# A hybrid encoder layer: another order of work at its start, and loads, stores and transposes moved around its far attention

## The chip, the cores and the metric

The kernel runs on one core of one Trainium2 chip. A core has a matrix engine (TensorE, here PE, with its weight loads as PEld), a vector engine (DVE), a scalar engine (ACT), GpSimd (POOL) and SyncE (SP); transfers are issued from the queues of SP, ACT and POOL and run on 16 DMA engines that they share. Every engine works through its own instructions in the order in which they were written, and waits for the others by semaphores. The metric is the device time of one execution in microseconds (us), as the median of several runs; less is better. Beside it stands one execution taken with the profiler, whose span and trace the text reads.

## The reference

One layer of an encoder over 2048 tokens of width 1024, with a memory of 256 tokens, all in float32:

```python
y = rmsnorm(h, norm_mix_g[l]) @ w_in[l]
q, k, v = ...                       # 8 heads of 64, partial rotary on q and k
att = dilated_sliding_attention(q, k, v)      # windows (128, 1), (512, 4), (2048, 16)
conv = conformer_conv(a, g, conv_w[l], conv_b[l], conv_ln_g[l], conv_ln_b[l])
                                    # a * sigmoid(g), 31 taps a channel, layernorm, silu
h = h + concatenate([att, conv]) @ w_out[l]
h = h + cross_attention(rmsnorm(h, norm_x_g[l]), rmsnorm(mem, norm_mem_g[l]))
h = h + square(relu(rmsnorm(h, norm_mlp_g[l]) @ w_up[l])) @ w_down[l]
return rmsnorm(h, norm_final_g)
```

The three outputs of the dilated attention are added with weights that come from their log denominators.

## The kernel before

**Arithmetic.** Each product of float32 matrices is made of three matmuls with a high and a low part of either side: high by high, high by low, low by high (`mm3`, L268 to L270). So each weight tile and each chunk of activations is split first: ACT casts the high part, DVE or POOL subtracts to get the low part. For the first stage these are f16 parts of weights that were scaled by a power of two; the scale comes from the sum of squares (`wscale`: ACT squares a 128x1024 tile at L207, PE adds over the partitions at L212, DVE works out the power of two), and `scaled_split` (L224 to L226) scales, casts and subtracts.

**The start (about 0 to 70 us).** `setup` (L154) loads seven small vectors in POOL's queue into one tile, `vecs`; PE transposes it (`pvec`, L163), and a short chain through DVE and PE (`pgain`, L254) gives `gmix`, the mixer's gain scaled by a power of two. `xprep` (L392) prepares 512 tokens of x, block n of four: it loads them in eight tiles (`xn`), ACT adds up their squares (`ssx`, L380), POOL and DVE make the reciprocal root (`rsx`), PE spreads it over the partitions (`rb`), ACT copies it (`rbs`, L400). Then for each of eight chunks of 128 columns PE transposes four tiles into a PSUM bank (`xt`, L405; two banks), DVE copies it (`xts`, L407; eight buffers) for a store to DRAM in SP's queue (`xscr`), DVE multiplies by gain and root (`xv`, L410; two buffers), ACT casts (`xh`) and POOL subtracts (`xl`). `glu_first` (L641) makes the first four units of the convolution's input from these chunks: g0, a0, g1, a1, each eight chunks by three matmuls of 512 columns. Its order is written by hand at the place where the stage is set up (L911 to L957): generators are advanced one step at a time, and a pin (`after`, `behind`, `pinned`) keeps an engine's next instructions behind a named earlier one. SP's queue also holds zeros for the edges of two DRAM tensors (`uscr`, `vtok`), the mask, and the next weights (`lraw`, `raw_v`).

**The linear stage (to about 400 us)** makes the rest of the gated units, q, k and v, and the convolution's first block on DVE.

**The far stage (about 400 to 700 us)** is the attention of the first 512 tokens with all three windows, four pairs of heads. Two windows' results go to DRAM (`oscr`), are loaded again (`ld`) and combined on DVE and POOL (`combine`, L1077 on). Between the attention's steps PE works through a list of other steps, `filler` (L1315): eight steps of the gated units of the later blocks at a time, and the folding of the cross attention's matrices (`Matrices`), where `turn` (L522) transposes weights of four heads on PE in four steps a head (`xqt`, L531), each copied by ACT and subtracted by DVE (`wlo_m`, L534).

**After it** comes the dense part: `wpost` (L1286) loads and splits the weights of the output projection (`raw_o`, `whi_o`, `wlo_o`; two raw buffers), of the cross attention and the MLP, while DVE and PE make the near attention of the next block.

Of the kernel before, what the change touches and what calls it, by code (L numbers as in the profile page):

```python
# [21 lines left out]
P = 128  # L22
# [25 lines left out]
def hybrid_layer(ctx, tc, A, out):  # L48
# [105 lines left out]
    def setup():  # L154
# [8 lines left out]
        PE.transpose(pv[:, 0:64], vecs, ident[0:64, 0:64])  # L163
        ACT.copy(gv, pv[:, 0:64])
        g8 = gv[:, GV["mix"]:GV["mix"] + 8]
# [3 lines left out]
        pg = ps("c", "pgain")  # L169
        bcast_rows(pg, top_[:, 0:1], 1)  # L170
        DVE.tensor_reduce(top_[:, 1:2], pg[:, 0:P], axis=AX.X, op=ALU.max)
# [4 lines left out]
        DVE.tensor_scalar(gmix, g8, top_[:, 4:5], None, op0=ALU.mult)  # L176

    def conv_weights():
        cwn = t2("cwn", F32, (32, DCONV))
        DVE.memset(cwn, 0.0)  # L180
# [42 lines left out]
    def scaled_split(raw, c, hi, lo, eng):  # L223
        ACT.activation(raw, raw, AF.Copy, scale=c)  # L224
        ACT.copy(hi, raw)
        eng.tensor_tensor(lo, raw, hi, op=ALU.subtract)  # L226
# [11 lines left out]
    def rstd_col(dst, ss_ps, n, stat):  # L238

        v = stat.tile([P, 8], F32, tag="st_v", name="st_v", bufs=2)  # L240
        t = stat.tile([P, 8], F32, tag="st_t", name="st_t", bufs=2)
        DVE.tensor_scalar(v[:, :n], ss_ps, 1.0 / D, EPS, op0=ALU.mult, op1=ALU.add)  # L242
        newton_rsqrt(dst, v[:, :n], t[:, :n])

    def newton_rsqrt(dst, v, t):
        POOL.tensor_tensor(dst, v, mhalf.to_broadcast([P, v.shape[1]]), op=ALU.pow)  # L246
        DVE.tensor_tensor(t, dst, dst, op=ALU.mult)
        DVE.scalar_tensor_tensor(t, t, -0.5, v, op0=ALU.mult, op1=ALU.mult)
        DVE.scalar_tensor_tensor(dst, t, 1.5, dst, op0=ALU.add, op1=ALU.mult)

    def bcast_rows(dst_ps, col, n):

        for j in range(n):
            PE.transpose(dst_ps[:, j * P:(j + 1) * P], col[:, j:j + 1].to_broadcast([P, P]), ident)  # L254

# [119 lines left out]

    def sumsq(sp, t, ss, j, n):

        for e in range(2):
            q = sp.tile([P, 512], BF16, tag="junk", name="junk", bufs=1)
            last["sumsq"] = ACT.activation(q, t[e], AF.Square, accum_out=ss[:, n * e + j:n * e + j + 1])  # L380

    def rstd_nat(sp, nat, name):
        n = len(nat)
        ss = sp.tile([P, 8], F32, tag="ss", name=f"ss{name}", bufs=2)
        for j in range(n):
            sumsq(sp, nat[j], ss, j, n)
        r = sp.tile([P, 4], F32, tag="rs", name=f"rs{name}", bufs=2)
        DVE.tensor_tensor(ss[:, 0:n], ss[:, 0:n], ss[:, n:2 * n], op=ALU.add)
        rstd_col(r[:, 0:n], ss[:, 0:n], n, sp)
        return r  # L390

    def xprep(sp, n):  # L392
        xtiles(n)
        nat = [load_nat(sp, A["x"][0, 512 * n + P * j:512 * n + P * (j + 1), :], f"xn{n}_{j}", q=nc.gpsimd if n > 1 else None) for j in range(4)]
        yield
        r = rstd_nat(sp, nat, f"x{n}")
        rb = ps("c", f"rb{n}")
        bcast_rows(rb, r, 4)
        rbs = sp.tile([P, 512], F32, tag="rbs", name=f"rbs{n}", bufs=1)
        ACT.copy(rbs, rb)  # L400
        yield
        for k in range(KC):
            pt = ps("a", f"xt{n}_{k}")
            for j in range(4):
                PE.transpose(pt[:, j * P:(j + 1) * P], nat_cols(nat[j], k), ident)  # L405
            xt = sp.tile([P, 512], F32, tag="xt", name=f"xts{n}_{k}", bufs=8)
            DVE.tensor_copy(xt, pt)  # L407
            dma(xscr[k][:, 512 * n:512 * (n + 1)], xt)
            xv = sp.tile([P, 512], F32, tag="xv", name=f"xv{n}_{k}", bufs=2)
            DVE.scalar_tensor_tensor(xv, pt, gmix[:, k:k + 1], rbs, op0=ALU.mult, op1=ALU.mult)  # L410
            last[f"x{n}_{k}"] = ACT.copy(XH_[k, n], xv)
            POOL.tensor_tensor(XL_[k, n], xv, XH_[k, n], op=ALU.subtract)
            yield
# [5 lines left out]
    def memory(sp):  # L419
# [23 lines left out]
        for i, t in enumerate((*mh, *ml)):  # L443
            dma(f(mscr[i]), f(t), nc.gpsimd)
        r = rstd_nat(sp, nat, "m")
        DVE.tensor_copy(rmem[:, 0:2], r[:, 0:2])
# [162 lines left out]
    def glu(c, ns, fine=False):  # L609
# [31 lines left out]
    def glu_first(sp, ns):  # L641
# [9 lines left out]
        for x, c in units:  # L651
# [3 lines left out]
                     for q in ("hi", "lo")]  # L655
            scaled_split(raw[nm], kept_scale[nm][0], *w[nm], POOL)
            if x == "a":
                DVE.tensor_scalar(cwu[:, c], cw[:, c], kept_scale[nm][1], None, op0=ALU.mult)
            yield
        for n in ns:  # L660
            for x, c in units:
# [3 lines left out]
                if x == "g":  # L665
                    sig = t2(f"sig{c}_{n}")
                    ACT.activation(sig, pt, AF.Tanh, scale=kept_scale[f"g{c}"][1])
                else:
                    u = t2(f"u{c}_{n}")
                    last["dve"] = DVE.scalar_tensor_tensor(u, sig, 1.0, pt, op0=ALU.add, op1=ALU.mult)  # L670
                    dma(uscr[c][:, 15 + 512 * n:15 + 512 * (n + 1)], u)
                yield
# [238 lines left out]
    with ExitStack() as st:  # L911
        sp = pool("stage", stack=st)
        setup()
        four = glu_first(sp, (0, 1))
# [8 lines left out]
        next(four)  # L923
        cwt = conv_weights()
        next(cwt)
        next(x0)
        behind("sumsq", four)
        drain(x0)
        with ExitStack() as st0:
            after(st0, "x0_3")  # L930
            drain(cwt)
        for _ in range(3):
            behind("x0_3", four)
        behind("x0_5", x1)
        for _ in range(6):
            behind("sumsq", four)
        early01 = (0, 1)
# [9 lines left out]
        steps = pipeline(*units, lin_v(hook), stage={0: 4})  # L947
        behind("x0_7", steps)
        drain(islice(steps, 6))
        weave(islice(steps, 24), (x1, 0.5))  # L950
        drain(x1)
        mem = memory(sp)
        later = pinned(chain(xprep(sp, 2), islice(mem, 1), xprep(sp, 3), mem), "x1_7")
        qks = pinned(qkscale(), "x1_7")
# [187 lines left out]
    def att_units(p, far, then):  # L1142
# [25 lines left out]
        def unit(pr, hh, pat, g, k, q_, opt, o0):  # L1168
# [139 lines left out]
    with ExitStack() as st:  # L1308
# [6 lines left out]
        def filler():  # L1315
# [691 lines left out]
```

## Time and profile before

| what | value |
|---|---|
| time, median of 3 runs | 2806.13 us (2802.68 to 2808.23) |
| the profiled execution's own time | 2799.84 us |
| its span | 2798.1 us |
| mean granted PE clock | 0.991 |
| busy: PE, DVE, ACT, POOL | 96%, 68%, 45%, 21% of the span |
| DMA | 535.68 MB, mean 191 GB/s |
| chain that ended last | PE 68%, issue 9%, DMA 8%, DVE 7%, ACT 3%, POOL 3%, SP's queue 2% |

The text reads the page, and from the trace a timeline (each row an instruction, or several alike, with its start, its duration, engine, line and operation, output and inputs; in brackets how long the engine was idle ahead of it and what ended that), a table of windows with each engine's busy time, and groups of instructions by line. A matmul's duration in a row reaches into the next one's, since they are pipelined: two matmuls of 512 columns whose rows say 0.38 start 0.215 us apart.

### The profile page before, as it was taken

How to read it: one execution, taken by the hardware profiler on the slowest of the kernel's cores; microseconds unless marked ns; L12 is line 12 of the kernel's file. 1: busy time of each engine (PE TensorE's matmuls, PEld its weight loads, DVE VectorE, ACT ScalarE, POOL GpSimd, SP SyncE). 2: the span in 40 equal slices, each digit the busy share in tenths (PEclk: the TensorE clock that was granted, in tenths of full speed). 3: DMA queues.
4: the chain of work that ended last, by engine and by line, in shares of the span. 5: the costliest groups of instructions: out<-in, count | busy, mean ns of one | idle time of the engine just before them, and what ended most of it. 6: DMA issues, size and time to landing. Idle time of an engine off the chain costs nothing.

```text
span 2798.1 us, 40584 instructions
## 1 busy us (share of the span) xinstructions
PE 2692.8 (96%) x14783; PEld 2072.3 (74%) x14783; DVE 1905.7 (68%) x3475; ACT 1271.6 (45%) x2171; POOL 583.6 (21%) x798
## 2 busy tenths in 40 slices
PE   6999999998899999999999999999999999999998
PEld 3544457876678888788888888887887788878887
DVE  4568826664689866578986578666475776666765
ACT  5842217655345333434544443454344444444435
POOL 5564313543002212200111201121010122100000
PEclk9999999999899999999999999999999999999999
DMA  9765557887535676767467766764534554584553
GB/s 273 209 184 114 142 165 203 245 240 226 174 120 185 199 233 201 236 217 218 139 190 222 254 207 217 234 235 136 165 124 132 188 199 150 174 300 152 165 184 106
DMA packets 468776, 535.68 MB, mean 191 GB/s; under 512 B 98172, under 2 KB 339440, under 8 KB 468576
## 3 DMA queue, kind: packets, MB, share of 16 engines
q1 hardware_dynamic: 431536, 412.03, 48.8%
q0 software_dynamic: 35312, 117.81, 11.8%
q10 hardware_dynamic: 1728, 3.24, 0.3%
q8 instruction: 116, 1.90, 0.3%
q14 instruction: 84, 0.69, 0.1%
HBM read 384.46 MB, written 148.52 MB: 190 GB/s over the span
## 4 chain that ended last, share of the span: by engine, by line
PE 68%; issue 9%; DMA 8%; DVE 7%; ACT 3%; POOL 3%; SPq 2%; POOLq 0%; ACTq 0%; DVEq 0%
PE b L1705 8%; PE dn L268 4%; PE dn L269 4%; PE dn L270 4%; PE up L268 3%; PE up L270 3%; PE up L269 3%; SPq L57 2%; PE lin L269 2%; PE lin L270 2%; PE lin L268 2%; PE pt L994 2%; PE s L1187 2%; PE x L269 1%; PE x L268 1%
## 5 line engine op out<-in xcount | busy, mean ns | idle before, releaser
L285 DVE SCALAR_TENSOR_TENSOR cacc<-cu,cwu,cacc 128x512 f32<-128x512 f32 x480 | 393.5, 821 | 6.4
L988 ACT ACTIVATE sm<-sm,o 128x256 f32<-128x256 f32 (+1 forms) x384 | 160.1, 467 | 118.3 <-DVE o L987 118.2
L268 PE MATMUL dn<-hhh,whi_d 128*128 128x512 f32 x512 | 201.9, 404 | 4.3 <-ACT hhh L1542 3.3
L268 PE MATMUL up<-mh,whi_u 128*128 128x512 f32 x512 | 203.9, 398 | 0.0
L269 PE MATMUL dn<-hhl,whi_d 128*128 128x512 f32 x512 | 200.7, 394 | 0.9 <-DVE hhl L1543 0.9
L270 PE MATMUL up<-mh,wlo_u 128*128 128x512 f32 x512 | 200.0, 391 | 0.0
L269 PE MATMUL up<-ml,whi_u 128*128 128x512 f32 x512 | 199.7, 390 | 0.0
L270 PE MATMUL dn<-hhh,wlo_d 128*128 128x512 f32 x512 | 199.6, 393 | 0.0
L987 DVE CUSTOM_DVE_ANT_0 sm<-s,mask 128x256 f32<-128x256 f32 (+1 forms) x384 | 126.9, 374 | 45.3 <-DMA oscr<-o 16.9
L246 POOL TENSOR_TENSOR nr<-st_v,mhalf 128x4 f32<-128x4 f32 x12 | 13.5, 1128 | 630.7 <-DVE st_v L242 630.7
L998 DVE TENSOR_TENSOR pl<-pt,ph 128x512 f16<-128x512 f32 x160 | 109.6, 685 | 49.6 <-ACT ph L997 49.2
L1557 DVE TENSOR_TENSOR h<-h,dn 128x512 f32<-128x512 f32 x128 | 86.4, 683 | 71.1 <-PE dn L270 70.7
L997 ACT CAST ph<-pt 128x512 f16<-128x512 f32 x160 | 92.6, 579 | 80.5 <-PE pt L994 79.9
L268 PEld LDWEIGHTS dn<-hhh,whi_d 128*128 128x128 f32 x512 | 95.6, 189 | 23.4 <-ACT hhh L1542 4.3
L270 PEld LDWEIGHTS dn<-hhh,wlo_d 128*128 128x128 f32 x512 | 96.7, 189 | 20.4
L269 PEld LDWEIGHTS dn<-hhl,whi_d 128*128 128x128 f32 x512 | 96.8, 189 | 19.7 <-DVE hhl L1543 1.8
L270 PEld LDWEIGHTS up<-mh,wlo_u 128*128 128x128 f32 x512 | 96.1, 188 | 20.5
L268 PEld LDWEIGHTS up<-mh,whi_u 128*128 128x128 f32 x512 | 96.2, 188 | 18.7
L269 PEld LDWEIGHTS up<-ml,whi_u 128*128 128x128 f32 x512 | 96.3, 188 | 18.5
L268 PE MATMUL o<-cath,whi_o 128*128 128x512 f32 x256 | 103.9, 406 | 5.2 <-ACT whi_o L259 4.5
L270 PE MATMUL o<-cath,wlo_o 128*128 128x512 f32 x256 | 102.2, 401 | 1.5 <-DVE wlo_o L260 1.5
L268 PE MATMUL x<-pth,whi_b 128*128 128x512 f32 x256 | 100.4, 398 | 2.4 <-ACT xp L1466 1.4
(622 smaller groups left out, 7982.1 us busy)
## 6 DMA issues: line engine op xcount, KB each, us to landing
raw_u<-in_w_up_dram SPq DMA_DIRECT2D x64, 512.0 KB
raw_d<-in_w_down_dram SPq DMA_DIRECT2D x64, 512.0 KB
k<-kscr SPq DMA_DIRECT2D x32, 640.0 KB
raw_a<-ascr SPq DMA_DIRECT2D x32, 512.0 KB
raw_b<-bscr SPq DMA_DIRECT2D x32, 512.0 KB
lou<-wlo_u POOLq DMA_DIRECT2D x32, 512.0 KB, 5.5
lod<-wlo_d POOLq DMA_DIRECT2D x32, 512.0 KB, 5.5
wlo_u<-lou SPq DMA_DIRECT2D x32, 512.0 KB
```

The lines of the kernel that those rows point to most:

```text
L57: (q or nc.sync).dma_start(o, i)
L268: PE.matmul(o, lh, rh, start=first, stop=False)
L269: PE.matmul(o, lh, rl, start=False, stop=False)
L270: last["pe"] = PE.matmul(o, ll, rh, start=False, stop=end)
L285: DVE.scalar_tensor_tensor(acc, u[:, t:t + 512], cwu[:, c, t:t + 1], acc, op0=ALU.mult, op1=ALU.add)
L987: last["dve"] = DVE.tensor_tensor_reduce(dst, so, mask[:, 256 * m:256 * m + nk], 1.0, 3e38, ALU.add, ALU.min, mn)
L988: last["act"] = ACT.activation(dst, dst, AF.Exp, bias=mn, scale=-1.0)
L994: last["pe"] = PE.transpose(pt[:, j, :], sm[:, j, :], ident)
L997: ACT.copy(ph, pt)
L998: DVE.tensor_tensor(pl, pt, ph, op=ALU.subtract)
L1557: last["dve"] = DVE.tensor_tensor(hs[m], hs[m], pt, op=ALU.add)
L1705: PE.matmul(o, w[i][:, k, :], Y[b][q][k], start=first and k + x == 0, stop=k == 3 and x == 2, skip_group_check=not first)
```

## The change

Four things are changed.

1. **The first 70 us.** The load of the convolution's weights (`cwn`) goes ahead of the vectors' loads. `gv` is copied by DVE, not ACT. The transposes of x's first chunks, and the root of x's first block, are pinned behind the vectors' chain, and DVE's copies `xts` behind `rsx0`. The low part of g0's weights is made by DVE, not POOL. The squares of x's second block are made in single steps between the chunks of the first. g0 and a0 go by turns over the chunks of the first block, in two PSUM banks, with the start of g1 between them; the scaled taps (`cwu`) follow a unit's end. The weights of the gated units that come next (`glu` with the first two blocks) are loaded in POOL's queue, not SP's; x's third block is loaded after the first block's last chunk. In SP's queue the zeros, the mask and `raw_v` thereby come ahead of all stores of x's first block.
2. **The last far store** (`oscr` of the fourth pair of heads) is issued by ACT, not SP.
3. **The output weights** 2 to 7 of the first block (`raw_o`) are loaded in POOL's queue, not SP's.
4. **The filler** takes two gated steps after each of the four steps of `turn`, where it took eight after the fourth.

The diff's core (the hand-written order at its end is cut):

```diff
-        ACT.copy(gv, pv[:, 0:64])
+        DVE.tensor_copy(gv, pv[:, 0:64])
...
+            with ExitStack() as st:
+                after(st, "rsx0")
+                DVE.tensor_copy(xt, pt)
...
-            dma(raw, wcols(w_in, c0), nc.gpsimd if fine else None)
+            dma(raw, wcols(w_in, c0), nc.gpsimd if fine or ns[0] == 0 else None)
...
-            scaled_split(raw[nm], kept_scale[nm][0], *w[nm], POOL)
+            scaled_split(raw[nm], kept_scale[nm][0], *w[nm], DVE if nm == "g0" else POOL)
...
+        pts = [ps("mm", f"lin{x}") for x in "ga"]
+        runs = [linear_steps(pts[i], *w[f"{x}0"], 0) for i, x in enumerate("ga")]
+        for i in (0, 0, 0, 0, 1, 0, 1, 1, 0, 1, 0, 1, 1, 0, 1, 1):
+            next(runs[i], None)
+            yield
+        for i, x in enumerate("ga"):
+            finish(x, 0, 0, pts[i])
...
+        cwt = conv_weights()
+        next(cwt)
         setup()
...
+        x0, x1 = pinned(x0, "pgain", "gain"), pinned(x1, "pgain", "gain")
         next(x0)
-        behind("sumsq", four)
+        behind("sumsq", pinned(four, "rsx0"))
...
-                    os_.rearrange("p b h e -> p b (h e)"), None if far else nc.scalar)
+                    os_.rearrange("p b h e -> p b (h e)"), None if far and pr < 3 else nc.scalar)
...
-        dma(raw, src)
+        dma(raw, src, nc.gpsimd if name[0:2] == "o0" else None)
...
-                yield from mats.turn(h)
-                yield from islice(gated, 8)
+                for _ in mats.turn(h):
+                    yield
+                    yield from islice(gated, 2)
```

PE's first rows before, from the last pair of x's first transposes on:

```order
L405 MATMUL xt_0_487<-ident,xn_3_0_402 128x128
L405 MATMUL xt_1_499<-ident,xn_3_0_402 128x128
L163 MATMUL pvec<-ident,vecs 128x64
L254 MATMUL pgain<-ident,gtop 128x128
L254 MATMUL rb_475<-ident,rsx_466 128x128 x4
L405 MATMUL xt_2_511<-ident,xn_0_0_390 128x128
```

And of the change, from PE's second row on:

```order
L213 MATMUL sqs_g_441<-sqv_g_439,small 128x1
L163 MATMUL pvec<-ident,vecs 128x64
L255 MATMUL pgain<-ident,gtop 128x128
L409 MATMUL xt_0_497<-ident,xn_0_0_392 128x128
L409 MATMUL xt_0_497<-ident,xn_1_0_396 128x128
L409 MATMUL xt_0_497<-ident,xn_2_0_400 128x128
```

`pvec` and `pgain` were behind the eight transposes of chunks 0 and 1, and are ahead of them now; `rb` follows those transposes.

ACT before, at about 43 to 54 us, where the root of x's second block (`rbs_636`) and the first weights of the next units (`lraw_g_669`, `lraw_a_681`) meet:

```order
L224 ACTIVATE fraw_a_434<-fraw_a_434,wscl 128x1024
L207 ACTIVATE sqj_a_694,sqv_a_695<-lraw_a_681 128x1024
L400 COPY rbs_636<-rb_631 128x512
L224 ACTIVATE lraw_g_669<-lraw_g_669,wscl 128x1024
L225 CAST fhi_a_663<-fraw_a_434 128x1024
```

And of the change, at the same place (`rbs_650`, `lraw_g_679`, `lraw_a_691`):

```order
L225 ACTIVATE fraw_a_436<-fraw_a_436,wscl 128x1024
L226 CAST fhi_a_674<-fraw_a_436 128x1024
L667 ACTIVATE sig_0_789<-ling,wscl 128x512
L667 ACTIVATE sig_0_856<-lin,wscl 128x512
L404 COPY rbs_650<-rb_645 128x512
L208 ACTIVATE sqj_g_681,sqv_g_682<-lraw_g_679 128x1024
L417 CAST xh_1_410<-xv_0_670 128x512
L208 ACTIVATE sqj_a_705,sqv_a_706<-lraw_a_691 128x1024
```

The root's copy stood behind a square that needs `lraw_a`, and stands ahead of both squares now.

SP's queue in the far stage, before, around the loads for the combine of the second pair of heads (`ld`; `v_02` are the values of the third pair):

```order
L57 DMA qh_5_6019<-qscr 64x2048
L57 DMA ql_3667<-qscr 64x2048
L57 DMA ld_6073<-oscr_2_89 128x4x132
L57 DMA ld_6073<-oscr_1_88 128x4x132
L57 DMA v_02_5999<-vtok 128x1x260 x5
```

And of the change:

```order
L57 DMA v_02_5999<-vtok 128x1x260 x7
L57 DMA ql_3667<-qscr 64x2048
L57 DMA v_02_5993<-vtok 128x1x260 x5
L57 DMA ld_6071<-oscr_1_88 128x4x132
L57 DMA ld_6071<-oscr_2_89 128x4x132
```

The two `ld` loads went behind five loads of values.

More of the change, by code (lines that the diff above doesn't have):

```diff
@@ L169, in setup @@
         pg = ps("c", "pgain")
-        bcast_rows(pg, top_[:, 0:1], 1)
+        last["pgain"] = bcast_rows(pg, top_[:, 0:1], 1)
         DVE.tensor_reduce(top_[:, 1:2], pg[:, 0:P], axis=AX.X, op=ALU.max)
@@ L224, in scaled_split @@
         ACT.activation(raw, raw, AF.Copy, scale=c)
-        ACT.copy(hi, raw)
+        last["split"] = ACT.copy(hi, raw)
         eng.tensor_tensor(lo, raw, hi, op=ALU.subtract)
@@ L374, in nat_cols, with sumsq, rstd_nat @@
         return t[k // 4][:, (k % 4) * P:(k % 4 + 1) * P]
[L376 to L382, printed above, removed]
+    def sumsq(sp, t, ss, j, n, e):
+        q = sp.tile([P, 512], BF16, tag="junk", name="junk", bufs=1)
+        last["sumsq"] = ACT.activation(q, t[e], AF.Square, accum_out=ss[:, n * e + j:n * e + j + 1])
+    def rstd_nat(sp, nat, name, steps=False):
         n = len(nat)
@@ L395, in xprep @@
         yield
-        r = rstd_nat(sp, nat, f"x{n}")
+        r = yield from rstd_nat(sp, nat, f"x{n}", n == 1)
         rb = ps("c", f"rb{n}")
-        bcast_rows(rb, r, 4)
+        last[f"rbt{n}"] = bcast_rows(rb, r, 4)
         rbs = sp.tile([P, 512], F32, tag="rbs", name=f"rbs{n}", bufs=1)
-        ACT.copy(rbs, rb)
+        last[f"rb{n}"] = ACT.copy(rbs, rb)
         yield
@@ L664, in glu_first @@
                     yield
[L665 to L671, printed above, removed]
+                finish(x, c, n, pt)
                 yield
```

78 lines of the change are left out of this document (53 added, 25 removed).

## The prediction

> **What bounds the kernel now.** The page's busy table comes first, then a table of windows (start:end, length, and for PE, PEld, DVE, ACT and POOL busy time with instruction count; then the granted PE clock, the DMA share and GB/s).
>
> ```profile
> PE 2692.8 (96%) x14783; PEld 2072.3 (74%) x14783; DVE 1905.7 (68%) x3475; ACT 1271.6 (45%) x2171; POOL 583.6 (21%) x798
> ```
> ```profile
> 0.00:20.00 20.00, 4.93 (x16) 2.74 (x16) 7.39 (x31) 10.88 (x23) 8.26 (x16) 1.00 0.95 325
> 20.00:40.00 20.00, 16.52 (x82) 9.76 (x83) 14.19 (x26) 15.47 (x33) 16.23 (x18) 1.00 0.97 213
> 40.00:60.00 20.00, 15.16 (x67) 6.56 (x65) 7.10 (x24) 11.81 (x20) 7.72 (x7) 0.91 0.77 258
> 240.00:400.00 160.00, 160.00 (x748) 73.23 (x746) 102.17 (x128) 34.77 (x46) 49.92 (x67) 1.00 0.46 126
> 400.00:640.00 240.00, 224.68 (x2172) 183.13 (x2171) 147.97 (x499) 145.29 (x323) 102.16 (x140) 0.99 0.81 236
> 700.00:740.00 40.00, 26.88 (x106) 19.71 (x106) 20.19 (x47) 12.48 (x20) 1.51 (x2) 0.79 0.61 180
> ```
>
> The span is 2798.1 us, so PE is idle for 2798.1 - 2692.8 = 105.3 us in all, and an edit that adds and removes no matmuls can only gain idle PE time or time at a low clock. In the first three windows PE is idle for 15.07 + 3.48 + 4.84 = 23.4 us; from 240 to 400 for none, so whatever is won before it passes straight through. In the far stage, 400 to 640, it is idle for 15.3 us with DMA at 0.81, and from 700 to 740 for 13.1 us with the clock at 0.79. The change touches these three places alone.
>
> **The start, part by part.** Rows of a timeline (start, duration, engine, line, operation; in brackets the idle time ahead of it and what ended it):
>
> ```profile
> 11.38 0.37 PE L163 MATMUL pvec<-ident,vecs 64*128 64x64 f32 x1
> 17.28 0.45 PE L254 MATMUL pgain<-ident,gtop 128*128 128x128 f32 x1 [5.53 <-DVE gtop L168]
> 18.11 1.12 PE L254 MATMUL rb<-ident,rsx 128*128 128x128 f32 x4 [0.39 <-DVE gtop L171]
> 20.78 1.94 PE L405 MATMUL xt<-ident,xn 128*128 128x128 f32 x8 [1.55 <-DVE xv L410]
> ```
> ```profile
> 14.88 1.97 DVE L249 SCALAR_TENSOR_TENSOR rsx<-st_t,rsx 128x4 f32<-128x4 f32 x1
> ...
> 18.65 0.23 DVE L176 TENSOR_SCALAR gmix<-gv,gtop 128x8 f32<-128x8 f32 x1
> ...
> 19.88 0.75 DVE L410 SCALAR_TENSOR_TENSOR xv<-xt,gmix,rbs 128x512 f32<-128x512 f32 x1 [0.69 <-ACT rbs L400]
> ```
> ```profile
> 13.41 1.04 POOL L246 TENSOR_TENSOR rsx<-st_v,mhalf 128x4 f32<-128x4 f32 x1 [8.06 <-DVE st_v L242]
> 14.72 2.12 POOL L226 TENSOR_TENSOR lwlo_g<-lraw_g,lwhi_g 128x1024 f16<-128x1024 f32 x1 [0.26 <-ACT lwhi_g L225]
> 17.95 0.59 POOL L57 DMA_DIRECT2D cwn<-in_conv_w_dram  x1 [1.11 <-DVE cwn L180]
> ```
>
> DVE's rsx step takes 1.97 us for four elements a row: it lies inside POOL's 2.12 us lwlo_g, ends with it, and the vectors' maximum stands behind it. Now I lay the new order out by hand with these durations. The cwn load goes out ahead of the vectors' loads: pvec at 11.38 + 0.59 = 12.0. Copy, square and maximum, about 0.2 us each, then 0.45 of pgain, then from the start of pgain to the end of gmix 18.88 - 17.28 = 1.6: gmix is done near 14.5, where it was done at 18.88. The rest of rsx follows: about 0.4 for back and st_v, 1.04 of pow, three steps of 0.2, near 16.7; rb 1.12 and its copy 0.6, near 18.5. DVE meanwhile does what POOL did (the same 1024-wide split, 1.23 us in DVE's wlo_m row below) and x0's two held copies (1.3), and reaches its first xv near 19.2 instead of 19.88. **First term: -0.7 us**, although the vectors themselves are 4 us earlier; what is late next is rsx.
>
> ```profile
> 32.32 0.39 PE L270 MATMUL lin<-xh,lwlo_a 128*128 128x512 f16 x1 [0.95 <-POOL lwlo_a L226]
> ...
> 45.58 0.39 PE L270 MATMUL lin<-xh,flo_g 128*128 128x512 f16 x1 [1.60 <-POOL flo_g L226]
> ...
> 53.52 1.29 PE L405 MATMUL xt<-ident,xn 128*128 128x128 f32 x8 [1.33 <-DVE xv L410]
> ...
> 56.83 0.39 PE L270 MATMUL lin<-xh,flo_a 128*128 128x512 f16 x1 [1.10 <-POOL flo_a L226]
> ```
>
> From 20.78 to 40 PE waits 3.48 - 0.78 = 2.7 us, for weights' sums and for low parts that POOL makes late. With two units by turns there is a second unit's matmul wherever one lacks its low part, and the low part of g1 comes a turn earlier. My schedule keeps one wait, 0.7 us near 28 for the sum of g1. **Second term: -2.0.**
>
> Of the 4.84 us from 40 to 60, 1.60 + 1.33 + 1.10 stand in the rows; the rest, 0.8, is short waits. In the new schedule the 1.60 and a short one (2.3) are replaced by two waits of about 1.0: for x1's rb, whose pow on POOL now stands behind eight loads of x2 (8 x 0.59 us to issue, as cwn's row), and for flo_a. That is -0.3. The clock of 0.91 is a loss of 20 x 0.09 = 1.8 us, behind the 1.60 us wait; I let it go, since no wait that long is left, and keep its return as a bound. **Third term: -2.1.** The Trainium skill, "TensorE: Matmul & The Clock Gate", Part 1, says that the clock falls only after an idle window of about 3.4 us. No wait that long stands ahead of this low clock; by the rule the third term would be -0.3 and the sum 1.8 us smaller, and by the row it is as I have it.
>
> The last two waits, 2.4 us, have one root:
>
> ```profile
> 50.96 1.06 ACT L207 ACTIVATE sqj_a<-lraw_a 128x1024 bf16<-128x1024 f32 x1 [6.02 <-DMA lraw_a<-in_w_in_dram]
> ```
> ```profile
> 37.41 5.06 SPq L57 DMA_DIRECT2D xscr<-xts  x3
> 42.56 0.77 SPq L57 DMA_DIRECT2D lraw_a<-in_w_in_dram  x1
> ```
>
> ACT stands 6.02 us for lraw_a, issued behind three stores of x in SP, and x1's rbs is queued behind it. In the new order rbs is ahead of these squares on ACT and the loads go out by POOL near 29. **Fourth term: -2.4**; PE is full from then on.
>
> A new wait is the price. SP now sends the zeros, the mask and raw_v ahead of x0's eight stores; x1's first copy takes the buffer of x0's first one, so DVE holds there until that store has landed, with x1's rsx and every xv behind it, and PE behind those. In my schedule DVE comes to that copy near 36, and a landing after 38 costs a us per us. Before, SP needed from 18.54 to 34.16 for the zeros and the weight beside them; started at 14.84 instead, that ends near 30.5. The mask and raw_v are 0.85 + 0.5 MB: at 325 GB/s they are through in 4.2 us, near 36; with the 1 MB of POOL's weight loads in between, at 258 GB/s, in 9, near 40. **Price: 0 to +3, and I take +1**, nearer the first, as x2's 2 MB no longer run there. The start sums to **-6.2 us**, from -10 (the whole schedule, waits under 0.2 us too, comes to -9.7) to -1 (the stores land late and the clock falls again).
>
> **The far stage.** Two things move against each other.
>
> ```profile
> L531 PE MATMUL xqt<-ident,raw_m 128*128 128x128 f32 x64 | 9.8, 276 | 6.5 <-DVE wlo_m L534 6.1 <-PE s L1187 0.4
> ```
> ```profile
> 557.63 1.25 SPq L57 DMA_DIRECT2D ld<-oscr  x2
> 558.98 7.43 SPq L57 DMA_DIRECT2D v<-vtok  x5
> ```
> ```profile
> 571.74 0.17 DVE L1098 TENSOR_TENSOR csm<-ld 128x8 f32<-128x8 f32 x1 [3.81 <-DMA ld<-oscr]
> ```
> ```profile
> 694.80 1.23 DVE L260 TENSOR_TENSOR wlo_m<-raw_m,whi_m 128x1024 fp32r<-128x1024 f32 x1 [2.03 <-ACT whi_m L259]
> ...
> 705.63 0.42 DVE L987 CUSTOM_DVE_ANT_0 sm<-s,mask 128x256 f32<-128x256 f32 x1 [9.61 <-DMA oscr<-o]
> ```
>
> The first row is the group of the turns over the whole stage (count, busy time and mean ns, then the idle time ahead): PE waits 6.5 us ahead of them, since the four of one head follow each other faster than DVE empties their banks. Spread between gated matmuls they find the bank empty: -4 to -6. But in SP the two ld loads of the second pair now stand behind five v loads, which SP needs 7.43 us to issue, and DVE, which already stands 3.81 us for the earlier ld, would stand up to 7.43 longer, with masks and low parts for PE queued behind. PE has a bank or two in hand, so I put it between +2 and +7; the middle cancels the gain. **Far stage: 0, from -5 to +7** (the whole 7, and turns that gain nothing).
>
> **The transition.** DVE's mask step waits 9.61 us for the last far store, which SP issues at 694.88 although ACT had its tile at 687.3.
>
> ```profile
> 688.46 6.30 SPq L57 DMA_DIRECT2D v<-vtok  x4
> 694.88 2.35 SPq L57 DMA_DIRECT2D oscr<-o  x1
> 697.28 6.99 SPq L57 DMA_DIRECT2D v<-vtok  x4
> ```
>
> From ACT's queue it goes out near 689 and the 9.61 us vanish for DVE. Yet the ld of that pair, which the combine and after it the output projection need, still stands behind eight v loads; it comes forward by the store's place, 0 to 2.35 us. The output weights on POOL wait only for their buffers, which takes away part of the low clock of 0.79, but share the engines with that ld. **Transition: -1.5, from -4 to 0.** The Trainium skill, "DMA: Bandwidth & Descriptors", Issuing engines are not separate DMA queues, says that another issuing engine saves only the time to initiate. By that rule the store's move is worth at most its 2.35 us row. The 6.30 us row ahead of it is a queue held by other loads, which the rule doesn't count; I weigh it as part of the first rival below.
>
> **Sum.** -6.2 + 0 - 1.5 = -7.7 us against the profiled execution's 2799.84 (span 2798.1 and 1.7 around it), 2792.1. That execution was 6.3 faster than the median of 2806.13, so the forecast beside the median is 2806.13 - 7.7 = **2798.4 us**. A measurement of this kernel can tell about 0.2%, 5.6 us, from no change.
>
> **Rivals.** *The start moves but not its end:* x0's stores land near 42 (+4 on my +1), the clock falls again (+1.8), the output weights fight with ld (transition 0). The start gives -1 to -4, the sum is within 0.2%: 2802 to 2806. For it speaks the DMA share of 0.95 and 0.97 up to 40 us; against it that x2's loads leave this stretch. Chance 0.22. *Slower:* the late ld in the far stage. If PE has no bank in hand it follows DVE fully and pays the 7.43, and pays it once more where the next pair's masks inherit the delay from the same DVE queue: 2 x 7.43 - 5 = +10 in this stage, and with a start of -1 and a transition of -1.5 the sum is +7.5, about 2814. It decides from the point where DVE stands over 11 us at that ld (3.81 + 7.43) and PE's wait behind it is as long. Against it: PE waited for under 2 us when DVE stood 3.81. Chance 0.13. *All of it:* the stores land by 36, the turns give 5 and the ld costs under 2: -10 - 3 - 3 = -16, about 2790. Chance 0.15. That leaves 0.50 for the forecast.
>
> The range takes in the ends of the three places: -10 - 5 - 4 = -19, 2787, and -1 + 7 + 0 = +6, 2812. Faster by over 0.2% has the forecast and the full gain, 0.65 less a little of the forecast's own edge: 0.64; within 0.2%: 0.22; slower: 0.14.
>
> **What would show it.** Right: PE idle from 0 to 60 near 17 us and the clock above 0.95 from 40 to 60; ACT without a wait over 2 us for lraw_a; rsx's last step back at 0.2 us; xqt's waits under 2 us in all; no 9.61 us wait for oscr. Wrong: a DVE row of xts with several us of waiting for xscr near 38; the csm row of the far stage's second pair waiting over 8 us; a PE gap of the same length elsewhere in 400 to 740. The forecast fails if 60 to 400 is no longer full of PE work, as then the start's gain doesn't pass through.

## The result, and the profile after

The median of the changed kernel is 2822.24 us (six runs, 2818.88 to 2828.28), beside 2805.4 of the kernel before on the same chip (six runs, 2799.62 to 2809.42): a ratio of 1.0061 [1.0045, 1.0077], so **17 us slower** [13, 22]. The forecast was 2798.4, with a range to 2812; it was wrong in sign. The profiled execution took 2822.83 us (span 2820.9, clock 0.985), 23 more than the profiled one of before, which was among the lower of its kind.

The page's busy table, and the table of windows with the same columns as before (one window, 120 to 160, is added):

```profile
PE 2697.3 (96%) x14783; PEld 2078.9 (74%) x14783; DVE 1904.4 (68%) x3477; ACT 1271.3 (45%) x2170; POOL 585.9 (21%) x807
```
```profile
0.00:20.00 20.00, 4.98 (x21) 4.29 (x22) 8.20 (x36) 12.48 (x26) 5.93 (x15) 1.00 0.94 318
20.00:40.00 20.00, 19.87 (x103) 11.53 (x102) 10.08 (x22) 14.95 (x32) 18.80 (x19) 1.00 0.94 189
40.00:60.00 20.00, 6.91 (x23) 2.83 (x22) 5.84 (x16) 6.21 (x9) 5.28 (x6) 0.60 0.81 306
120.00:160.00 40.00, 33.03 (x161) 17.07 (x160) 26.51 (x44) 24.34 (x28) 18.05 (x19) 0.92 0.69 180
240.00:400.00 160.00, 160.00 (x748) 73.06 (x746) 109.81 (x140) 38.12 (x50) 56.26 (x76) 1.00 0.45 124
400.00:640.00 240.00, 218.45 (x2026) 175.62 (x2025) 136.89 (x461) 136.01 (x301) 95.85 (x132) 0.97 0.78 217
700.00:740.00 40.00, 27.21 (x159) 20.53 (x158) 18.12 (x49) 19.63 (x34) 11.84 (x15) 0.84 0.89 297
```

PE's idle time from 20 to 40 us is nearly gone (0.13 us, 3.48 before). But from 40 to 60 it is idle for 13.1 us instead of 4.84, and the clock there is 0.60 instead of 0.91. In the added window the kernel before has this row, with PE idle for 0.63 us and a full clock, against 6.97 and 0.92 now:

```profile
120.00:160.00 40.00, 39.37 (x200) 19.66 (x198) 22.82 (x30) 25.83 (x32) 18.19 (x23) 1.00 0.72 207
```

Rows of after's timeline, first PE, then DVE, then SP's queue:

```profile
11.52 0.34 PE L163 MATMUL pvec<-ident,vecs 64*128 64x64 f32 x1 [5.16 <-DMA vecs<-in_norm_final_g_dram]
...
19.46 1.94 PE L409 MATMUL xt<-ident,xn 128*128 128x128 f32 x8 [1.82 <-DVE xv L416]
...
53.33 0.61 PE L270 MATMUL lin<-xh,fhi_a 128*128 128x512 f16 x1 [11.42 <-ACT fhi_a L226]
...
155.33 1.94 PE L440 MATMUL mt<-ident,mn 128*128 128x128 f32 x8 [5.47 <-DVE mlo L447]
```
```profile
47.79 0.69 DVE L413 COPY xts<-xt 128x512 f32<-128x512 f32 x1 [13.65 <-DMA xscr<-xts]
...
587.45 0.17 DVE L1133 TENSOR_TENSOR csm<-ld 128x8 f32<-128x8 f32 x1 [3.77 <-DMA ld<-oscr]
...
732.79 0.17 DVE L1133 TENSOR_TENSOR csm<-ld 128x8 f32<-128x8 f32 x1 [11.27 <-DMA ld<-oscr]
```
```profile
14.93 3.65 SPq L57 DMA_DIRECT2D uscr<-zero  x2
18.68 1.33 SPq L57 DMA_DIRECT2D vtok<-zrow  x2
20.06 12.59 SPq L57 DMA_DIRECT2D uscr<-zero  x6
32.69 0.47 SPq L57 DMA_DIRECT2D mask<-in_masks_dram  x1
33.21 0.44 SPq L57 DMA_DIRECT2D raw_v<-in_w_in_dram  x1
33.75 16.84 SPq L57 DMA_DIRECT2D xscr<-xts  x10
```

The start is right up to 40 us: the first xv comes earlier (PE resumes at 19.46, before at 20.78). Then DVE stands 13.65 us for x0's first store, and PE, whose next matmul needs a cast that ACT makes behind DVE's work, stands 11.42. That is the row that the prediction named as the one that would show it wrong. The DMA view of after from 20 to 60 us, in 40 slices of 1 us (busy share in tenths, then GB/s), shows why the store landed at 47.8:

```profile
DMA  9888898889878999979999999999999931052894
GB/s 144 100 100 100 100 100 100 100 100 100 108 155 336 327 277 332 279 214 315 400 397 402 411 422 400 423 410 410 422 391 406 369 131 64 10 231 51 243 365 158
```

While the two zero stores to `vtok` (520 KB each) run, to about 31 us, the engines are at 0.8 to 0.9 and move 100 GB/s. Behind them, from 31 to 47.8 (where DVE's wait for the store ends), the slices add up to 5.8 MB: the mask, raw_v (together 1.4 MB) and x0's first stores in SP's queue, and in POOL's three weight loads (1.6) and about 1.6 of the 2.1 MB of x2's eight loads. A store that was issued at 33.75 shares the engines with all that is in flight.

Two places that the prediction hadn't looked at follow: the gap of 5.47 us at 155, and, in the far stage, the groups of the turns and of the folding that follows them, of before and of after:

```profile
L268 PE MATMUL pa<-kt,whi_m 128*128 128x256 f32 x64 | 19.1, 299 | 1.0 <-ACT sig L632 1.0
```
```profile
L270 PE MATMUL pa<-kt,whi_m 128*128 128x256 f32 x64 | 20.6, 321 | 4.8 <-DVE wlo_m L540 4.8
...
L537 PE MATMUL xqt<-ident,raw_m 128*128 128x128 f32 x64 | 10.4, 287 | 5.0 <-ACT sig L638 4.8
```

The turns' waits for wlo_m (6.1 of 6.5 us) became waits for the gated units' sigmoid (4.8) and, one matmul later, for wlo_m (4.8).

To see where time is lost, two traces are laid side by side: for each PE instruction the start in the other kernel less the start of the same one before, and the median over a stretch of before's time. Above zero is later than before, and the ladder rises where time is lost. The trace of before behind it is 5 us under its median, and single traces scatter by some us, so its steps are read and not its end.

```
stretch (us)        85-100 150-170 300-350 450-480 575-610 655-675 750-800
after                 5.6    13.8    11.1    11.9    21.1    17.9    19.4
e1_start              4.3    11.7     7.0     9.8     9.6     5.2     5.8
e2_filler            -1.0    -0.8    -0.4    -0.5     7.8     4.1     5.0
e3_queues            -0.9    -0.2    -0.2     0.5     2.2    -1.3     0.2
e4_zeros_late         2.1     9.9     5.9     6.8    17.0    12.8    17.1
e5_root_first       -10.4     2.7    -2.7     0.1     2.6    -1.9     0.5
e6_casts_order       -9.2    -5.9   -10.0    -8.9    -6.4   -10.9    -9.9
e7_turn_2_8_2        -1.3    -1.4    -1.5    -1.4    -1.0    -1.7    -1.4
e8_store              1.2     1.7     1.9     2.0     3.9     0.1     1.3
e9_whole_mended     -10.3    -7.2   -11.9   -11.4    -2.3    -5.0    -3.6
e10_zeros_early       1.3    11.9     7.4     7.9    11.1     7.8     7.7
e11_turn_other_bank  -1.1    -0.5     0.0     0.1     7.7    10.1    11.6
```

After loses time at three steps: 5.6 us by 85, 8.2 more by 150, and some 9 in the far stage.

### The profile page after: what moved, and what is told of

It reads as the page before. It is cut to its first block, busy times and chain, and to the rows that moved or that the text cites. A ratio compares the mean times of both kernels' runs of the same rounds, so it can differ in the third digit from the quotient of the medians.

```text
span 2820.9 us, 40578 instructions
## 1 busy us (share of the span) xinstructions
PE 2697.3 (96%) x14783; PEld 2078.9 (74%) x14783; DVE 1904.4 (68%) x3477; ACT 1271.3 (45%) x2170; POOL 585.9 (21%) x807
## 4 chain that ended last, share of the span: by engine, by line
PE 68%; DMA 10%; issue 8%; DVE 7%; ACT 3%; POOL 2%; SPq 2%; POOLq 0%; ACTq 0%; DVEq 0%
PE b L1741 7%; PE dn L270 4%; PE dn L271 4%; PE dn L272 4%; PE up L270 3%; PE up L272 3%; PE up L271 3%; PE lin L272 2%; PE lin L271 2%; PE lin L270 2%; SPq L57 2%; PE pt L1029 2%; PE s L1222 1%; PE x L271 1%; PE x L270 1%
```

## The experiments

The main theory (A where an expectation uses letters) is that these steps are separate and add up: the start loses by the wait for x0's stores, the filler by its order, the queues by nothing. The rival (B) is that one of them drives the others, or that the cause within a step is another resource than the one named in the row. The kernel before ran beside each group: 2805.19 us (33 runs) for e1 to e4, 2805.16 (35) for e5 to e8, 2803.88 (29) for e9 to e11. A gain or loss in us is the measured ratio's, with its interval in brackets; the plain difference of the two medians lies up to 3.4 us off it (9.0 us for e1 beside 6.7), which is within the intervals.

**e1_start**: part 1 of the change alone. The edit is against the kernel after; those of e2, e3, e7 and e8 are against the one before.

```diff
-                    os_.rearrange("p b h e -> p b (h e)"), None if far and pr < 3 else nc.scalar)
+                    os_.rearrange("p b h e -> p b (h e)"), None if far else nc.scalar)
...
-        dma(raw, src, nc.gpsimd if name[0:2] == "o0" else None)
+        dma(raw, src)
...
-                for _ in mats.turn(h):
-                    yield
-                    yield from islice(gated, 2)
+                yield from mats.turn(h)
+                yield from islice(gated, 8)
```

> Only the first part of the change (the first 70 us); the last far store, the output weights and the filler as before. Theory A: the time is lost here, where DVE waits 13.7 us for x's first stores in the changed kernel; the ladder of equal PE instructions stands at +11 us from 240 to 400 us there, so this kernel should be 9 to 13 us slower than the one before, with the same 11.4 us gap on PE near 42. Rival B: the loss comes from the far stage and the transition (the ladder goes from +12 to +21 between 520 and 600); then this kernel is within 4 us of the one before, and the start's loss is made up later.

Measured: 2814.23, ratio 1.0024 [1.0010, 1.0038], 6.7 us [3, 11] slower, under the 9 to 13 expected (9.0 by medians, at their edge). The wait for the store is there as in after (14.17 us on DVE, 11.92 on PE), and so are the ladder's first two steps.

**e2_filler**: before, with part 4 alone.

```diff
-                yield from mats.turn(h)
-                yield from islice(gated, 8)
+                for _ in mats.turn(h):
+                    yield
+                    yield from islice(gated, 2)
```

> The kernel before with the filler's change alone (two gated steps after each of turn's four steps). My forecast had the turns' 6.5 us of waits go and an ld of 7 us come. The changed kernel shows another price: waits of PE for the gated units' sig on ACT ahead of xqt (4.8 us), and for wlo_m ahead of pa. Theory A: +5 to +9 us. Rival: 0, if what those rows cost is what the old waits cost.

Measured: 2811.61, 1.0016 [1.0003, 1.0028], 4.5 us [1, 8] slower, just under what was expected. Groups of e2 by line in the far stage, and then the two PE rows with the worst of its waits:

```profile
L268 PE MATMUL pa<-kt,whi_m 128*128 128x256 f32 x64 | 20.7, 323 | 4.8 <-DVE wlo_m L534 4.8
...
L531 PE MATMUL xqt<-ident,raw_m 128*128 128x128 f32 x64 | 10.4, 287 | 5.0 <-ACT sig L632 4.8
```
```profile
551.79 0.66 PE L531 MATMUL xqt<-ident,raw_m 128*128 128x128 f32 x4 [2.35 <-ACT sig L632]
...
553.85 0.58 PE L268 MATMUL pa<-kt,whi_m 128*128 128x256 f32 x1 [1.40 <-DVE wlo_m L534]
```

These are the waits of after to a tenth, in a kernel whose start is that of before: the filler's order alone makes them.

**e3_queues**: before, with parts 2 and 3 alone.

```diff
-                    os_.rearrange("p b h e -> p b (h e)"), None if far else nc.scalar)
+                    os_.rearrange("p b h e -> p b (h e)"), None if far and pr < 3 else nc.scalar)
...
-        dma(raw, src)
+        dma(raw, src, nc.gpsimd if name[0:2] == "o0" else None)
```

> The kernel before with the last far store on ACT's queue and the output weights 2 to 7 on POOL's. Theory A: DVE's 9.6 us for the store is replaced by a wait for ld of about as long, and PE's 7.6 us by one for v: between -1 and +2 us. My forecast's term was -1.5. Rival: the three MB of output weights that start earlier hold up ld and v, and it costs 3 us or more.

Measured: 2806.54, 1.0007 [0.9997, 1.0017]: no gain. Rows of DVE and of PE at the transition:

```profile
714.92 0.17 DVE L1098 TENSOR_TENSOR csm<-ld 128x8 f32<-128x8 f32 x1 [11.59 <-DMA ld<-oscr]
```
```profile
715.14 0.21 PE L1002 MATMUL opt<-v,ph 128*128 128x65 f16 x1 [9.20 <-DMA v<-vtok]
```

The 9.61 us wait for the store is gone, and the wait for the ld that follows it in SP's queue, 1.31 us before, is 11.59. The three parts sum to 6.7 + 4.5 + 2.0 = 13.2 us, at the lower end of after's 13 to 22, and each of them is known to some 4 us; by differences of medians they sum to 9.0 + 6.4 + 1.4 = 16.8 beside 16.8. So the runs agree with steps that add up, within this noise.

**e4_zeros_late**: the whole change, with the zeros made by DVE behind the last xv of x's first block, so that their stores go out behind x0's.

```diff
+    cpad = cst.tile([P, 48], F32, name="cpad")
...
-        DVE.memset(zrow, 0.0)
+        with ExitStack() as st:
+            after(st, "xv0_7")
+            DVE.memset(zrow, 0.0)
+            DVE.memset(cpad, 0.0)
...
-            dma(uscr[c][:, 0:15], zero[:, 0:15])
-            dma(uscr[c][:, 15 + S:2080], zero[:, 0:17])
+            dma(uscr[c][:, 0:15], cpad[:, 0:15])
+            dma(uscr[c][:, 15 + S:2080], cpad[:, 0:17])
```

> The whole change, with the zeros of the edges (two stores of 520 KB, eight of 7.5 or 8.5 KB) written by DVE only after x0's last chunk, so that they stand behind x0's stores in SP's queue. Theory A: x1's first copies find their buffers free; the 13.7 us wait of DVE and PE's 11.4 us gap go, and the time falls by 9 to 15 us against the changed kernel. Rival C: the stores land late because of the mask and of POOL's loads, not of the zeros: under 4 us better.

Measured: 2814.69, 1.0032 [1.0021, 1.0043], 7.5 us less than after by medians, where 9 to 15 were expected. No wait for a store is left, yet PE stands as long. Rows of e4's POOL and PE, with the row of after's POOL for the same load last:

```profile
48.94 0.54 POOL L57 DMA_DIRECT2D xn<-in_x_dram  x1 [8.38 <-issue]
49.49 1.04 POOL L247 TENSOR_TENSOR rsx<-st_v,mhalf 128x4 f32<-128x4 f32 x1
```
```profile
53.19 1.09 PE L255 MATMUL rb<-ident,rsx 128*128 128x128 f32 x4 [11.28 <-DVE rsx L250]
```
```profile
44.24 0.54 POOL L57 DMA_DIRECT2D xn<-in_x_dram  x1 [3.28 <-issue]
```

POOL stands 8.38 us at the issue of x2's eighth load, and the power for x1's root is queued right behind it. A second block had run beside the first, hidden by it. The mending also makes it longer, for the zeros now run beside x2's loads. The DMA view of e4 from 20 to 60 us, in slices of 1 us, has 77 to 114 GB/s in each slice from 33 to 45:

```profile
GB/s 327 306 345 395 373 369 305 264 18 131 381 336 363 109 114 100 100 100 100 77 98 98 98 96 83 314 369 404 410 421 379 410 346 153 32 216 341 266 166 272
```

The power runs at 37.24 in e5 below, where nothing holds it, and at 49.49 here, 12.3 us later. In after POOL was through with x2's loads at 44.78, so the hidden block there was at most 7.5 us.

The traces also tell when POOL goes on. Its transfers report their landing by eight semaphores in turn, and in none of the 13 traces (some 5,100 issues) does one begin before the transfer eight places ahead of it has landed. For x2's eighth load that is the third weight load: it lands at 48.41 in e4, at 43.71 in after and at 41.97 in e1, and in each the load goes out 0.53 to 0.54 us later.

**e5_root_first**: e1 with the zeros late, and x2's loads pinned behind x1's root and a1's low part on POOL.

```diff
+        last[f"pow{n}"] = last["pow"]
...
+            last[f"lo{nm}"] = last["lo"]
...
-        later = pinned(chain(xprep(sp, 2), islice(mem, 1), xprep(sp, 3), mem), "x1_7", "xl0_7")
+        later = pinned(chain(xprep(sp, 2), islice(mem, 1), xprep(sp, 3), mem), "x1_7", "xl0_7", "pow1", "loa1")
```

> The first part of the change alone, with the zeros late as in e4, and with x2's eight loads in POOL's queue pinned behind the pow of x1's root and the low part of a1. In e4 the store's wait was gone, but POOL stood 8.4 us at the issue of x2's eighth load, the pow stood behind it, and PE waited 11.3 us for rb. Theory A: both blocks were in parallel, and with both gone PE has no wait over 3 us from 20 to 60; the ladder at 75 to 100 us, +4.3 in e1, comes to between -4 and -8, and the time is 5 to 10 us under e1's. Rival: the queue stays full, and what stands behind x2's loads next (x1's low parts xl) holds PE as long: ladder within 3 us of e4's +2.

Measured: 2800.63, 0.9984 [0.9969, 0.9999], 4.5 us faster than before. The ladder stands at -10.4 by 85 us, beyond the -4 to -8 expected. Two rows of its windows:

```profile
40.00:60.00 20.00, 20.00 (x108) 10.70 (x106) 9.81 (x19) 9.81 (x17) 15.40 (x19) 1.00 1.01 292
120.00:160.00 40.00, 31.84 (x151) 15.85 (x150) 20.38 (x23) 22.05 (x27) 19.88 (x23) 0.91 0.63 192
```

PE is full from 40 to 60 at a full clock; but by 150 the ladder has risen by 13 us again. There ACT's order differs. Its rows of before and of after, whose order e5 has too (134.19 and 135.24 for the two rows):

```profile
135.30 4.77 ACT L802 CAST lwhi_qr<-lraw_qr 128x512 f16<-128x512 f32 x2
...
142.48 1.15 ACT L224 ACTIVATE lraw_q<-lraw_q,qkc 128x1024 f32<-128x1024 f32 x1 [1.85 <-DMA lraw_q<-in_w_in_dram]
```
```profile
145.18 1.15 ACT L225 ACTIVATE lraw_q<-lraw_q,qkc 128x1024 f32<-128x1024 f32 x1 [2.29 <-DMA lraw_q<-in_w_in_dram]
...
146.74 4.71 ACT L818 CAST lwhi_qr<-lraw_qr 128x512 f16<-128x512 f32 x2
```

The scaling of the next weights, which waits for its load, has moved ahead of the casts of the rotary weights; DVE's low parts wait for those casts (5.16 us in after, 4.99 in e5), and PE's transposes of the memory (`mt`) behind DVE (5.47 and 5.59).

**e6_casts_order**: e5, with that scaling pinned behind the casts.

```diff
+                last[f"hi{nm}"] = ACT.copy(hv, rv)
...
+            with ExitStack() as st:
+                after(st, "hiqr")
+                scaled_split(raw, sc, hi, lo, POOL)
```

> e5 with one pin more: on ACT the scaling of the next k and q weights, which waits for their loads, stands behind the casts of the rotary parts (lwhi_kr, lwhi_qr), as before the change. In e1 the ladder rises by 7.9 us at 149, where PE waits 5.5 us for mlo, DVE 5.2 us for lwhi_qr, and ACT for lraw_q's load and x3's chunks. Theory: the order on ACT costs most of that step: the rise between 125 and 175 falls to 4 us or less. Rival: the step comes from x3's chunks being late, whatever ACT's order: the rise stays 6 us or more.

Measured: 2792.18 (2787.76 to 2796.22), 0.9961 [0.9950, 0.9972]: **11 us faster than before**, the best version here. Its window:

```profile
120.00:160.00 40.00, 38.05 (x192) 18.91 (x191) 22.56 (x25) 25.79 (x33) 22.67 (x26) 1.00 0.73 211
```

PE's idle time is 1.95 us where e5 had 8.16, and the clock is full. The ladder rises by 3.3 us to 150, not by 13.

**e7_turn_2_8_2**: before, with the eight gated steps in one piece between the second and third step of the turn.

```diff
-                yield from mats.turn(h)
+                turn = mats.turn(h)
+                yield from islice(turn, 2)
                 yield from islice(gated, 8)
+                yield from turn
```

> The kernel before, with the filler as two steps of turn, eight gated steps, two steps of turn. Two PSUM banks serve the gated units and xqt. Theory: in the changed filler an open gated unit holds one of the two banks over its eight steps, so xqt waits for sig (4.8 us); here the eight gated steps stay together and those waits go, but turn's last step stands right ahead of score, so the waits of pa for wlo_m stay: xqt's waits for sig under 1 us, time within 4 us of before. Rival: the sig waits are ACT's lateness and stay.

Measured: 2806.75, 1.0004 [0.9990, 1.0018]. Two rows of its groups:

```profile
L268 PE MATMUL pa<-kt,whi_m 128*128 128x256 f32 x64 | 19.4, 304 | 3.5 <-issue 1.5 <-DVE wlo_m L534 1.1 <-PE xqt L531 0.7
...
L531 PE MATMUL xqt<-ident,raw_m 128*128 128x128 f32 x64 | 9.9, 277 | 0.0
```

The turns' waits are gone. `pa` behind them waits 3.5 us where it waited 1.0, of which 1.1 for wlo_m, so both together fall from 7.5 to 3.5 us (the expectation had pa's waits for wlo_m stay), and the time is the same.

**e8_store**: before, with part 2 alone (the first line of e3's diff).

> The kernel before with the last far store in ACT's queue alone. Forecast's mechanism: DVE's 9.6 us wait for the store goes. Theory: the next thing late is ld behind eight loads of v in SP's queue: DVE waits for ld instead, and the ladder from 750 on is between -3 and +1. With e3 it tells what the output weights on POOL add.

Measured: 2804.34, 1.0003 [0.9988, 1.0018]. Its rows of DVE and PE at the transition:

```profile
713.75 0.17 DVE L1098 TENSOR_TENSOR csm<-ld 128x8 f32<-128x8 f32 x1 [7.96 <-DMA ld<-oscr]
```
```profile
713.99 0.21 PE L1002 MATMUL opt<-v,ph 128*128 128x65 f16 x1 [4.02 <-DMA v<-vtok]
```

By one trace of each, e3's wait is 11.59 - 7.96 = 3.6 us longer; the output weights in POOL's queue are all that e3 has beside e8.

**e9_whole_mended**: the whole change with the three mendings of e5 and e6 (zeros late, root first, casts first).

> The whole change with the three mendings of e6 (zeros late, x1's root and a1's low part ahead of x2's loads on POOL, casts ahead of the next scaling on ACT). If the parts add up, it is e6's time plus what the filler (+4.4) and the queues (+1.3) cost by themselves: 2792 + 6 = 2798 us, 2794 to 2802. Rival: the far stage shifted by the start hides its own price, or the parts overlap: under 2794.

Measured: 2800.28, 0.9975 [0.9961, 0.9988], 7 us faster than before and, by medians, 22 less than after, inside the 2794 to 2802 expected. The ladder falls to -11.4 before the far stage and gives back 8 to 9 in it.

**e10_zeros_early**: e5 with the zeros where the change has them (e5's edit of the zeros undone).

> e5 with the zeros where the change has them, ahead of x0's stores in SP's queue: POOL's order as in e5, no late zeros. Theory: the two blocks were in parallel, so the wait for the stores alone still holds DVE at x1's first copy by 10 us or more, PE idles about 11 us near 42, and the ladder at 75 to 100 stays at +2 to +5, as in e1. Rival: POOL's order was the whole of it, and the ladder falls to -8 as in e5.

Measured: 2807.87, 1.0009 [0.9996, 1.0023]. DVE's and PE's waits and the ladder's 1.3 are below the 10, 11 and 2 to 5 us expected. Rows of its DVE and PE:

```profile
43.51 1.32 DVE L414 COPY xts<-xt 128x512 f32<-128x512 f32 x2 [9.84 <-DMA xscr<-xts]
```
```profile
46.95 1.09 PE L255 MATMUL rb<-ident,rsx 128*128 128x128 f32 x4 [5.53 <-DVE rsx L250]
```

With x2's loads out of the way the store lands at 43.5, 4.3 us sooner than in after, and PE stands half as long; the clock from 40 to 60 us is 0.74 (0.66 in e1, 1.00 in e5). e1, e4, e5 and e10 make a square, by the ladder at 85 to 100 (e4's other parts act only later): both blocks 4.3, x2's loads alone 2.1, the zeros alone 1.3, neither -10.4. Each of the two middle runs lies about 12 us above the last, the first 15. But the 12 of x2's loads are e4's, with the moved zeros beside them, and a block of x2's loads without zeros in flight was not run. At the end of the whole run less is left: by the ratios e10 is 7 us and e1 11 us behind e5.

**e11_turn_other_bank**: e2, with the turns' transposes in the banks of the attention's transposes.

```diff
-                    pt = ps("mm", f"xqt{i}{g}")
+                    pt = ps("T", f"xqt{i}{g}")
```

> e2 (the change's filler alone) with the turned weights xqt in the two PSUM banks of the attention's transposes, not in the two that the gated units use. Theory: xqt waited for sig because an open gated unit holds one of its two banks; here xqt's waits for sig fall from 4.8 to under 1 us, and the ladder's rise between 525 and 600 (+7.9 in e2) falls below +5, unless pt now waits. Rival: no change of the rise (within 1.5 us).

Measured: 2812.58, 1.0024 [1.0008, 1.0040]. Rows of its groups:

```profile
L994 PE MATMUL pt<-ident,sm 128*128 128x128 f32 x228 | 37.9, 284 | 7.8 <-DVE pl L998 3.3 <-ACT sm L988 2.8 <-DVE ctl L1137 1.6
...
L268 PE MATMUL pa<-kt,whi_m 128*128 128x256 f32 x64 | 20.9, 326 | 0.0
...
L531 PE MATMUL xqt<-ident,raw_m 128*128 128x128 f32 x64 | 9.9, 277 | 0.4 <-DVE wlo_m L534 0.4
```

xqt's wait for the sigmoid vanishes with the other bank, which shows that the bank was what it waited for, and pa's wait for wlo_m goes with it; but the attention's transposes (`pt`), 0.9 us before, now wait 7.8. One window over the far stage's work, of before, of e2 and of e11, tells what that costs:

```profile
480.00:660.00 180.00, 165.46 (x1625) 131.73 (x1625) 110.88 (x388) 102.25 (x243) 80.21 (x121) 0.98 0.79 229
```
```profile
480.00:660.00 180.00, 164.01 (x1585) 132.10 (x1586) 108.17 (x377) 99.68 (x236) 79.20 (x121) 0.96 0.78 224
```
```profile
480.00:660.00 180.00, 162.89 (x1524) 130.67 (x1523) 103.61 (x358) 97.25 (x227) 75.78 (x117) 0.93 0.83 225
```

e2 has 1.5 us more idle time on PE, and at most 180 x 0.02 = 3.6 us by the clock (two digits, and a low clock costs nothing while PE is idle): up to 5.1, where its ladder rises by 4.6 from 450 to 675. e11 has 2.6 and at most 180 x 0.05 = 9: up to 11.6, where its ladder rises by 10.0. The same window shows the clock in the other traces: 0.94 to 0.96 in the four kernels with the change's filler (after, e2, e4, e9), 0.98 or 0.99 in the eight without it.

## Why the prediction was wrong, point by point

- **First term (-0.7).** Right in mechanism, with 20.78 - 19.46 = 1.3 us instead of 0.7.
- **Second term (-2.0).** Better than forecast: PE lacks 0.13 us from 20 to 40, not the 0.7 that I left.
- **Third and fourth term (-2.1 and -2.4).** Not to be seen in after, since the gap lies over them. e5 shows them: PE full from 40 to 60, clock 1.00, no wait for lraw_a. The whole gain of the start is the ladder's -10.4 in e5 and -9.2 in e6, beside my -9.7 for the whole schedule.
- **The price of the new wait (+1, 0 to +3): the step that failed.** I had the wait and its place, but x0's first store landed at 47.8 and not between 36 and 40. The zeros' issue ended at 32.65, 2 us later than I put it. More weighs that I counted 1.35 to 2.35 MB ahead of that store and said that x2's 2 MB no longer run there: they were issued from 37.19 on, and 5.8 MB moved from 31 us until the store had landed (without x2's loads, in e10, it landed 4.3 us sooner). I set the delay as if transfers ended in the order of issue. A second block, POOL's stand at x2's eighth load with the power behind it, I priced by eight issues of 0.59 us, 4.7 us; POOL needed 7.6 in after (37.19 to 44.78) and 12.7 in e4. The square of four runs gives 15 us for both blocks together. So the first rival's mechanism was the right one for the start, but the two blocks cost 15 us where the rival had +5.
- **"60 to 400 is no longer full of PE work".** This condition of failure came true, by a cause that I had not foreseen: ACT's order at 145 us changed although the change edits nothing there, and PE stands 5.47 us. I had compared the orders of the engines only where the diff pointed. e6 against e5 gives 8.4 us of medians for that one pin. So "the change touches these three places alone" was wrong too.
- **Far stage (0, -5 to +7).** Measured +4.5 [1, 8] (e2): the middle was 4.5 us off, the range held. Both halves of the working were wrong. The turns do not find the bank empty: between their steps a gated unit holds one of the banks until its sigmoid. And the late ld cost nothing that shows, 3.77 us of waiting against 3.81, though SP issues it behind more loads of v; so the slower rival fell as a mechanism, although the kernel came out slower. The larger part of the loss in this stage is the clock (up to 3.6 of 5.1 us), which I had not priced here. In e2 no single wait is over 2.5 us, but the 2.35 and 1.40 us have only one group of transposes, 0.66 us, between them, and the slice from 540 to 560 has a clock of 0.91 where before has 1.00. The Trainium skill, "TensorE: Matmul & The Clock Gate", Part 1, has a free-running activity window of about 3.4 us. The prediction read it as a rule on single waits, and two waits close together that sum to 3.75 us bear it out better than that reading. How much idle time in one window suffices stays open: the low clock of before at 40 to 60 us stands behind a wait of 1.60 us.
- **Transition (-1.5, -4 to 0).** Measured +0.8 us [-3, 5] for the store and +2.0 [-1, 5] with the weights: nothing that can be told from zero. The wait for the store became the wait for ld (7.96 us in e8, 11.27 in after), which stands in SP's queue behind the loads of v as before. The Trainium skill, "DMA: Bandwidth & Descriptors", Issuing engines are not separate DMA queues, lets such a move save only the time to initiate. e8's time agrees, and the sentence should have had my term's place.
- **The sum.** e6's gain with e2's and e3's losses, -10.9 + 4.5 + 2.0 = -4.4 us, is what the change would be with its two accidents taken away; e9 measured -7.0 [-10.9, -3.4]. The forecast of -7.7 is near the time of that kernel, not of the one that was made, and that it is so near is luck: the start gave 4.7 us more than my -6.2, the far stage and the transition 4.5 and 3.5 less than my 0 and -1.5.

Open: how long x2's loads would hold x1's root with no zeros in flight was not tried. And what remains of after's 17.1 over the parts' 13.2 is within the scatter of both.

## What to carry to other kernels

A wait that is moved from one queue to another is priced by all bytes in flight when its transfer runs, not by those issued ahead of it, and it may hide a second block: take away each alone and both together before trusting either, and look whether the mending of one lengthens the other. Compare the engines' orders of before and after to the end of the stretch through which a gain must pass, not only where the diff points. Steps put between others share their accumulation banks, so ask of each interleaving which bank is still held by a sum that is not finished.

## What the runs showed of the hardware that was not expected

The two zero stores of 520 KB, taken from 16 partitions, keep the DMA engines at 0.8 to 0.9 busy for about 10 us at 100 GB/s, where the stretch behind them moves up to 423; six further stores of 7.5 and 8.5 KB keep SP's queue from 20.06 to 32.65. The kernel before has the same stretch, 94 to 100 GB/s from 23 to 31 us, so it could have been read ahead of the result. POOL's queue stood up to 8.38 us at the issue of one load, with one load of 512 KB and seven of 256 KB of its own under way (e4), until the first of these eight had landed. And the gap of 11.42 us cost more than its length. Three windows of after behind it:

```profile
53.00:58.00 5.00, 3.01 (x9) 1.43 (x10) 2.15 (x5) 2.28 (x5) 2.12 (x1) 0.50 0.38 120
58.00:63.00 5.00, 5.00 (x17) 1.94 (x16) 1.18 (x2) 2.85 (x6) 2.31 (x2) 0.68 0.31 105
63.00:68.00 5.00, 5.00 (x30) 2.93 (x29) 3.75 (x10) 3.32 (x5) 3.21 (x5) 1.00 0.35 106
```

The clock is at half when the work begins again: matmuls of 512 columns start 0.43 us apart up to 61.2, and 0.215 behind that. PE worked for 3.0 of the first five us, so the loss is 3.0 x 0.50 + 5 x 0.32 = 3.1 us beside the gap.
